# Stores of chunk preparation from GpSimd, and half of the retention's gate columns behind the z columns

## The chip, the cores and the metric

The kernel runs on one core of a Trainium2 chip. It is one program with one launch. The metric is the time of one execution on the device, in microseconds; the number compared is the median over runs. The engines are named TensorE (PE), VectorE (DVE), ScalarE (ACT), GpSimd (POOL) and SyncE (SP); SP computes nothing and only issues transfers.

## The reference

One layer of a diffusion backbone over 1024 latent tokens with 256 context tokens ahead of them, width 1024, all in float32:

```python
h = concat([modulate(rms_norm(ctx)), modulate(rms_norm(x))])          # 1280 tokens
p = h @ w_in                                                          # 4112 columns
qkv_a, z, ab, rq, rk, rv, rg = split(p)
qkv_a = silu(short_conv(qkv_a))                                       # 5 taps, q/k/v of the delta rule
q, k = l2_normalize(q) * 128 ** -0.5, l2_normalize(k)
o_gdn = rms_norm(delta_rule(fwd) + delta_rule(bwd)) * silu(z)         # 4 heads of 128, chunks of 64
o_ret = head_group_norm(retention(fwd) + retention(bwd)) * silu(rg)   # 4 heads of 128, rotary on rq, rk
x = x + g1 * (concat([o_gdn, o_ret])[latent] @ w_out)
x = x + g2 * swiglu(modulate(rms_norm(x)))
return rms_norm(x, final_g)
```

Inside the delta rule each chunk needs the solution of a unit lower triangular system:

```python
decay = where(incl, exp(G[i] - G[j]), 0)            # G: cumulated log gates of the chunk
A   = where(strict, (k * beta) @ k.T * decay, 0)
sol = triangular_solve(A + I, rhs)                  # per chunk, head and direction
qk  = (q @ k.T) * decay
```

The gate columns rg (512 of them) and z (512) are needed only behind the scans, as silu(rg) and silu(z).

## The kernel before

The kernel works on tiles of 128 tokens: 2 of the context and 8 of the latents, numbered 0 to 9, each with 4 heads and 2 directions. Matrix products of float32 are made of three products of a high and a low part (`whi`, `wlo`, `hhi`, `hlo`).

The stages in program order that matter here:

- **Column-major convolutions** (`conv_block`, matmuls in L611 to L613 into `b`, taps in L621 on VectorE, SiLU in L624 on ScalarE). One call makes 128 columns: blocks 4 to 7 are k, 0 to 3 are q, 8 to 11 are v. Between them `ada_rest` computes the rest of the adaLN vector. Its last calls write the gate rows with `SY.dma_start(grow[...], row)` (L506), behind an addition on VectorE (L505).
- **Token-major groups** (`token_major(g, ...)`, matmuls in L371 to L373 into `tm`). One group is 256 columns; groups 6 and 7 are the two halves of rg, groups 8 and 9 are z. Each works through the 8 latent tiles: 24 matmuls of 128x256 for a tile, then a finish on ScalarE (`fin_gate`, L532) and a store (L387). The weights of a group are two loads of 512 KB, split by ScalarE (L344) and VectorE (L345). Groups 6 and 7 take their weights from pool `W2` with loads issued by SyncE, groups 8 and 9 from pool `W` with loads issued by ScalarE. Behind `W2` come the pools of the next stage (`GU`, `GI`, `GP`), in the memory that it leaves.
- **Chunk preparation** (`pre(t)`). For a tile: load k (`kc`), its products (`kk`, L705), for latent tiles also q (`qc`), its transposes (`qt`) and products (`kq`, L715). For each direction ("a half" in what follows): load the broadcast gates (`gw`, two buffers, L718), cut them by an affine select on GpSimd (`e`, L722), four Exp on ScalarE (L726), the products `ut` and for latent tiles `sp` on VectorE (L730, L732), an Exp of `gw` (L735) and the product `sp` on GpSimd (L736), and two stores: `un<-ut` (L733) and `sd<-sp` (L737), both from SyncE.
- **Inversion** (`invert(b)`), for batches of 4, 4 and 2 tiles: load the 32x32 diagonal blocks (`yr`, L751), then 31 steps of two VectorE instructions each (L765, L767) on `X`, a transposing copy (`XT`, L769) and four stores to `xd`.
- **Merges** (`merge(b)`): load `U` and `t` (L783 to L788), then small matmuls (L807 to L834) that put the 32x32 inverses together to 128x128.
- v convolutions (each with transposes `vT`, L856, and scaled copies `vt`, L859) stand in the program between the solves of batches 0 and 1 and the preparation of batch 2; groups 8 and 9 follow merge 2; the scans come behind them.

The program order isn't the order on the engines. A scheduler orders the instructions of all engines ahead of time, by dependences, priorities and its own times, and each engine then runs its list strictly in order. So a change in the program moves instructions on every engine. All DMA issues are part of such a list too: an issue that waits holds up everything behind it on its engine.

```python
BATCH = [[0,1,2,9],[3,8,4,7],[5,6]]
```

## Time and profile before

| | us |
|---|---|
| median of 3 runs | 1476.58 (1475.48 to 1484.42) |
| the profiled execution | 1477.96 |
| its span | 1476.2 |
| TensorE busy | 1397.2 (95%) |
| VectorE busy | 964.6 (65%) |
| ScalarE busy | 614.0 (42%) |
| GpSimd busy | 590.3 (40%) |

The page splits the span into 40 slices of 36.9 us; a digit is the busy share of the slice in tenths. A row of the windows gives the stretch, its length, the busy time of the engines named (with the count of instructions), the granted clock of TensorE as a share of full speed, the busy share of the DMA engines and the GB/s. A row of the timeline gives the start in us, the length in us, the engine, the line, the operation, what it writes and reads, and in brackets how long the engine stood idle ahead of it and what ended that. A row of groups gives busy time and mean ns, then the idle time ahead of these instructions and what ended most of it. A row of waits gives the instruction that waited, what it waited for, the us in total, how often and the longest.

### The profile page before, as it was taken

How to read it: one execution, taken by the hardware profiler on the slowest of the kernel's cores; microseconds unless marked ns; L12 is line 12 of the kernel's file. 1: busy time of each engine (PE TensorE's matmuls, PEld its weight loads, DVE VectorE, ACT ScalarE, POOL GpSimd, SP SyncE). 2: the span in 40 equal slices, each digit the busy share in tenths (PEclk: the TensorE clock that was granted, in tenths of full speed). 3: DMA queues.
4: the chain of work that ended last, by engine and by line, in shares of the span. 5: the costliest groups of instructions: out<-in, count | busy, mean ns of one | idle time of the engine just before them, and what ended most of it. 6: DMA issues, size and time to landing. Idle time of an engine off the chain costs nothing.

```text
span 1476.2 us, 24111 instructions
## 1 busy us (share of the span) xinstructions
PE 1397.2 (95%) x8919; PEld 1199.2 (81%) x8919; DVE 964.6 (65%) x1856; ACT 614.0 (42%) x1326; POOL 590.3 (40%) x501
## 2 busy tenths in 40 slices
PE   7999999986789999899799899999999999999997
PEld 2898888975689999898688688877888888788885
DVE  6566789289792435689676877556555564657477
ACT  5643564587333111245443623233333332444445
POOL 0120010243202344234144688898555552335321
PEclk9999999998899999999899999999999999999999
DMA  9536686688888625996532265674222242776863
GB/s 337 197 105 205 189 249 200 219 264 277 282 216 277 238 76 178 416 341 209 184 125 104 97 238 210 242 264 162 105 97 105 107 151 79 260 260 194 288 216 114
DMA packets 170421, 298.14 MB, mean 202 GB/s; under 512 B 43496, under 2 KB 93880, under 8 KB 165952
## 3 DMA queue, kind: packets, MB, share of 16 engines
q1 hardware_dynamic: 118752, 253.17, 50.2%
q10 hardware_dynamic: 49072, 35.83, 7.8%
q0 software_dynamic: 2480, 7.60, 1.4%
q8 instruction: 70, 1.15, 0.3%
q14 instruction: 47, 0.39, 0.1%
HBM read 206.60 MB, written 89.96 MB: 201 GB/s over the span
## 4 chain that ended last, share of the span: by engine, by line
PE 55%; POOL 6%; DMA 5%; DVE 4%; issue 2%; ACT 2%; SPq 1%; ACTq 0%; POOLq 0%; DVEq 0%
PE ffn L1344 7%; PE ffn L1342 6%; PE ffn L1343 6%; PE fo L1470 4%; PE fo L1469 4%; PE fo L1468 4%; PE tm L371 3%; PE tm L373 3%; PE tm L372 3%; PE op L1203 2%; PE op L1201 2%; PE op L1202 2%; DMA wd<-tw 2%; POOL ws L1315 1%; DMA pk<-sd 1%
## 5 line engine op out<-in xcount | busy, mean ns | idle before, releaser
L371 PE MATMUL tm<-whi,hhi 128*128 128x256 f32 (+1 forms) x704 | 199.5, 287 | 7.7 <-ACT vt L859 3.4
L372 PE MATMUL tm<-wlo,hhi 128*128 128x256 f32 (+1 forms) x704 | 199.3, 285 | 2.4 <-issue 2.0
L373 PE MATMUL tm<-whi,hlo 128*128 128x256 f32 (+1 forms) x704 | 197.7, 285 | 0.0
L371 PEld LDWEIGHTS tm<-whi,hhi 128*128 128x128 f32 x704 | 132.8, 190 | 11.8 <-ACT vt L859 3.6
L1342 PE MATMUL ffn<-t,whi 128*128 128x512 f32 x352 | 136.9, 390 | 1.3 <-ACT whi L344 1.3
L1344 PE MATMUL ffn<-t,wlo 128*128 128x512 f32 x352 | 137.0, 390 | 1.0 <-DVE wlo L345 1.0
L1343 PE MATMUL ffn<-t,whi 128*128 128x512 f32 x352 | 137.0, 389 | 0.0
L372 PEld LDWEIGHTS tm<-wlo,hhi 128*128 128x128 f32 x704 | 133.7, 190 | 2.1 <-issue 0.9
L373 PEld LDWEIGHTS tm<-whi,hlo 128*128 128x128 f32 x704 | 132.8, 190 | 2.6 <-issue 1.8
L344 ACT ACTIVATE whi<-wraw 128x512 fp32r<-128x512 f32 (+2 forms) x98 | 75.1, 771 | 141.4 <-PE ffn L1343 80.5
L344 ACT ACTIVATE whi<-ws 128x512 fp32r<-128x512 f32 x88 | 55.6, 632 | 171.5 <-PE ffn L1343 123.4
L345 DVE TENSOR_TENSOR wlo<-ws,whi 128x512 fp32r<-128x512 f32 x88 | 93.9, 1068 | 47.0 <-ACT whi L344 46.8
L1469 PE MATMUL fo<-wlo,ahi 128*128 128x512 f32 x308 | 120.2, 390 | 2.1 <-DVE wlo L345 2.1
L1468 PE MATMUL fo<-whi,ahi 128*128 128x512 f32 x308 | 119.3, 390 | 0.7 <-ACT ahi L344 0.7
L1470 PE MATMUL fo<-whi,alo 128*128 128x512 f32 x308 | 119.0, 390 | 0.0
L345 DVE TENSOR_TENSOR wlo<-wraw,whi 128x512 fp32r<-128x512 f32 (+2 forms) x92 | 99.4, 1082 | 24.6 <-ACT whi L344 24.6
L1342 PE MATMUL ffn<-b,whi 128*128 128x512 f32 x264 | 103.8, 393 | 4.4 <-ACT whi L344 4.4
L1344 PE MATMUL ffn<-b,wlo 128*128 128x512 f32 x264 | 103.6, 393 | 0.8 <-DVE wlo L345 0.8
L1343 PE MATMUL ffn<-b,whi 128*128 128x512 f32 x264 | 103.4, 392 | 0.0
L612 PE MATMUL b<-hlo,whi 128*128 128x512 f32 (+1 forms) x256 | 94.4, 369 | 0.0
L613 PE MATMUL b<-hhi,wlo 128*128 128x512 f32 (+1 forms) x256 | 94.3, 368 | 0.0
L611 PE MATMUL b<-hhi,whi 128*128 128x512 f32 (+1 forms) x256 | 94.3, 368 | 0.0
(446 smaller groups left out, 3448.1 us busy)
## 6 DMA issues: line engine op xcount, KB each, us to landing
adaw<-ada SPq DMA_DIRECT2D x48, 512.0 KB, 4.4
pk<-sd SPq DMA_DIRECT2D x16, 1536.0 KB, 10.0
wraw<-wfi SPq DMA_DIRECT2D x44, 512.0 KB, 3.7
ar<-ad SPq DMA_DIRECT2D x33, 512.0 KB, 4.7
w<-wfo SPq DMA_DIRECT2D x22, 512.0 KB, 5.7
wd<-tw SPq DMA_DIRECT2D x11, 1024.0 KB, 4.8
ad<-act SPq DMA_DIRECT2D x20, 512.0 KB, 3.0
raw<-wd SPq DMA_DIRECT2D x20, 512.0 KB, 4.9
```

Source lines behind the costliest of these rows:

```text
L344: S.activation(hi, raw, AF.Copy)
L345: e.tensor_tensor(lo, raw, hi.bitcast(F32), ALU.subtract)
L371: T.matmul(o, hhi[:, k, tsl], whi[:, k % 4, :], start=(k == 0), stop=False)
L372: T.matmul(o, hhi[:, k, tsl], wlo[:, k % 4, :], start=False, stop=False)
L373: T.matmul(o, hlo[:, k, tsl], whi[:, k % 4, :], start=False, stop=(k == KT - 1))
L612: T.matmul(o, whi[:, k, :], hl, start=False, stop=False)
L1342: T.matmul(o, whi[:, k, :], xhi(xn, slice(0, 4), k), start=(first and k == 0), stop=False, **kw)
L1343: T.matmul(o, whi[:, k, :], xlo(xn, slice(0, 4), k), start=False, stop=False, **kw)
L1344: T.matmul(o, wlo[:, k, :], xhi(xn, slice(0, 4), k), start=False, stop=(k == 3), **kw)
L1468: T.matmul(po[g][i], ahi[:, ts], whi, start=(j == 0 and not kw), stop=False, **kw)
L1469: T.matmul(po[g][i], ahi[:, ts], wlo, start=False, stop=False, **kw)
L1470: T.matmul(po[g][i], alo[:, ts], whi, start=False, stop=(j == FH - 1), **kw)
```

## The change

Three things are changed. The gate row store of `ada_rest` is issued by GpSimd instead of SyncE. In `pre`, both stores of a half of a latent tile (t >= 2; 16 halves) are issued by GpSimd, behind its product `sp`; the stores of the 4 halves of the two context tiles stay on SyncE. Group 7, the second half of rg, leaves its place behind group 6, ahead of the chunk preparation, and follows groups 8 and 9; with that its weights come from pool `W`, loaded from ScalarE's queue.

```diff
@@ ada_rest
                 V.tensor_tensor(row, row, ps[:1, :], ALU.add)
-                SY.dma_start(grow[0 if c == 2 else 1][:, half * 512:(half + 1) * 512], row)
+                G.dma_start(grow[0 if c == 2 else 1][:, half * 512:(half + 1) * 512], row)
@@ behind the q convolutions
         checkpoint("q")
-        for g in (6, 7):
-            token_major(g, LAT, fin_gate, S, W2, SY)
+        token_major(6, LAT, fin_gate, S, W2, SY)
         checkpoint("rg")
@@ pre
-                SY.dma_start(un[b][:, 1 - d, c * H:(c + 1) * H, :], ut)
-                if t >= 2:
+                if t < 2:
+                    SY.dma_start(un[b][:, 1 - d, c * H:(c + 1) * H, :], ut)
+                else:
                     S.activation(gw, gw, AF.Exp)
                     G.tensor_tensor(sp[:, 1], gw, qc, ALU.mult)
-                    SY.dma_start(sd[t, :, 8 - 8 * d:10 - 8 * d], sp.rearrange("p a h i -> p a (h i)"))
+                    G.dma_start(un[b][:, 1 - d, c * H:(c + 1) * H, :], ut)
+                    G.dma_start(sd[t, :, 8 - 8 * d:10 - 8 * d], sp.rearrange("p a h i -> p a (h i)"))
@@ behind merge 2
-        for g in (8, 9):
+        for g in (8, 9, 7):
             token_major(g, LAT, fin_gate, S, W)
```

What this moves in the lists of three engines, at one place each. VectorE where the q convolutions end and the chunk preparation begins, before (`y` are taps, `row` is the gate row, `ut` and `sp` the products of preparation):

```order
L621 SCALAR_TENSOR_TENSOR y<-u,cw,y 128x254
L505 TENSOR_TENSOR row<-row,gr 1x512
L730 TENSOR_TENSOR ut<-kk,e 128x512 x6
L732 TENSOR_TENSOR sp<-kq,e 128x512 x2
L345 TENSOR_TENSOR wlo<-wraw,whi 128x8x128
L621 SCALAR_TENSOR_TENSOR y<-u,cw,y 128x1022
```

and the same place now:

```order
L505 TENSOR_TENSOR row<-row,gr 1x512
L345 TENSOR_TENSOR wlo<-wraw,whi 128x8x128
L621 SCALAR_TENSOR_TENSOR y<-u,cw,y 128x1022
L621 SCALAR_TENSOR_TENSOR y<-u,cw,y 128x1023
L621 SCALAR_TENSOR_TENSOR y<-u,cw,y 128x254
L621 SCALAR_TENSOR_TENSOR y<-u,cw,y 128x1023
L621 SCALAR_TENSOR_TENSOR y<-u,cw,y 128x255
L621 SCALAR_TENSOR_TENSOR y<-u,cw,y 128x1022
L621 SCALAR_TENSOR_TENSOR y<-u,cw,y 128x255
L729 TENSOR_TENSOR ut<-kk,e 128x512 x2
```

The taps of the first v convolution stand ahead of the first `ut` now. (Lines behind L684 are one lower or one higher in the new text.)

GpSimd in the preparation of the second batch, before (`e` is the affine select, `sp` the product):

```order
L722 AFFINE_SELECT e<-gw 128x512
L736 TENSOR_TENSOR sp<-gw,qc 128x512
L722 AFFINE_SELECT e<-gw 128x512 x2
L736 TENSOR_TENSOR sp<-gw,qc 128x512 x2
L722 AFFINE_SELECT e<-gw 128x512
```

and now, with the stores of `ut` and `sp` in its list:

```order
L721 AFFINE_SELECT e<-gw 128x512 x2
L736 TENSOR_TENSOR sp<-gw,qc 128x512
L737 DMA un_2657<-ut 128x512
L738 DMA sd<-sp 128x1024
L736 TENSOR_TENSOR sp<-gw,qc 128x512
L737 DMA un_2657<-ut 128x512
L721 AFFINE_SELECT e<-gw 128x512
L738 DMA sd<-sp 128x1024
L721 AFFINE_SELECT e<-gw 128x512
```

An affine select stands behind the stores of the half or two halves ahead of it.

TensorE where merge 2 begins, before (`m1` and `m2` are merge matmuls; `tm_5543` is a tile of the group behind z, all of groups 6 to 9 is done):

```order
L372 MATMUL tm_5543<-wlo_5537,hhi_86 128x256
L834 MATMUL m2_4772<-U1_4550,xt2_4773 64x64 x16
L807 MATMUL m1_4825<-t64_4815,U2_4813 32x32 x32
L373 MATMUL tm_5543<-whi_5536,hlo_87 128x256
L371 MATMUL tm_5543<-whi_5536,hhi_86 128x256
```

and now (`tm_5316` and `tm_5317` are the fifth and sixth of the 8 tiles of group 7):

```order
L371 MATMUL tm_5317<-whi_5192,hhi_86 128x256
L835 MATMUL m2_4536<-U1_4314,xt2_4537 64x64 x16
L808 MATMUL m1_4589<-t64_4579,U2_4577 32x32 x32
L372 MATMUL tm_5317<-wlo_5193,hhi_86 128x256
L373 MATMUL tm_5317<-whi_5192,hlo_87 128x256
```

Group 7 stands between the merges now, and what stood there comes behind merge 2.

## The prediction

> **What bounds the kernel now.** I read the page first, then busy time by stretch, then the stretch around the change on each engine, then what SyncE waits for.
>
> The page, its span and the two rows of the 40 slices for TensorE and its clock:
>
> ```profile
> span 1476.2 us, 24111 instructions
> PE 1397.2 (95%) x8919; PEld 1199.2 (81%) x8919; DVE 964.6 (65%) x1856; ACT 614.0 (42%) x1326; POOL 590.3 (40%) x501
> PE   7999999986789999899799899999999999999997
> PEclk9999999998899999999899999999999999999999
> ```
>
> TensorE is busy 95% of the span, so a change can win only what TensorE stands idle, or lose by making idle time. The weak slices are numbers 9 to 11 and the clock falls with them: 295 to 405 us. That is the chunk preparation. By 40 us:
>
> ```profile
> core 0: us, PE busy (x) PEld busy (x) DVE busy (x) ACT busy (x) POOL busy (x), PEclk, DMA share, GB/s
> 240.00:280.00 40.00, 40.00 (x299) 37.45 (x298) 21.01 (x41) 17.73 (x34) 6.80 (x9) 1.00 0.54 166
> 280.00:320.00 40.00, 38.17 (x232) 32.86 (x231) 25.93 (x33) 31.94 (x94) 15.26 (x14) 1.00 0.89 282
> 320.00:360.00 40.00, 31.54 (x186) 26.77 (x184) 39.48 (x60) 34.40 (x92) 18.73 (x16) 0.97 0.82 255
> 360.00:400.00 40.00, 25.56 (x188) 24.97 (x189) 31.38 (x68) 16.23 (x52) 10.02 (x8) 0.81 0.88 297
> 400.00:440.00 40.00, 34.45 (x891) 32.55 (x889) 37.02 (x97) 11.94 (x21) 0.95 (x1) 0.96 0.87 204
> 440.00:480.00 40.00, 37.77 (x636) 36.01 (x637) 12.93 (x35) 12.28 (x23) 7.81 (x17) 1.00 0.86 282
> 480.00:583.00 103.00, 103.00 (x879) 102.69 (x879) 44.40 (x138) 11.76 (x16) 45.77 (x91) 1.00 0.42 154
> ```
>
> TensorE's idle time from 280 to 480 us is 1.83 + 8.46 + 14.44 + 5.55 + 2.23 = 32.5 us; before (240 to 280) and after (480 to 583) there is none. So 32.5 us, and a few more for the clock of 0.81 and 0.96, is all the change can win. VectorE is full in 320 to 360 and nearly so in 400 to 440: its chain (preparation, inversion of three batches, merges) sets the pace, and TensorE waits for it.
>
> **What leaves the front.** TensorE and VectorE where group 7 ends and preparation begins:
>
> ```profile
> 276.06 0.28 PE L372 MATMUL tm<-wlo,hhi 128*128 128x256 f32 x1
> 276.17 0.28 PE L373 MATMUL tm<-whi,hlo 128*128 128x256 f32 x1
> 276.29 1.95 PE L705 MATMUL kk<-kc 128*128 128x128 f32 x16
> 261.10 0.68 DVE L505 TENSOR_TENSOR row<-row,gr 1x512 f32<-1x512 f32 x1 [1.84 <-PE gr L504]
> 277.48 1.29 DVE L730 TENSOR_TENSOR ut<-kk,e 128x512 f32<-128x512 f32 x2 [15.70 <-POOL X L755]
> 276.51 1.84 POOL L755 MEMSET X<- 128x1024 f32 x2 [7.06 <-PE tm L373]
> 268.53 2.46 ACT L726 ACTIVATE e<-e,nG 128x128 f32<-128x128 f32 x8 [1.46 <-POOL e L722]
> ```
>
> Group 7 is 8 token tiles x 8 k x 3 = 192 matmuls, 0.12 us apart: 23.0 us. While they run VectorE does nothing for 15.7 us, though the first two decay tiles e stand ready at 268.53 + 2.46 = 270.99; the first kk is queued behind group 7, and GpSimd's clearing of X (in memory that group 7's weights held) waits for it too, with the third decay tile behind it.
>
> In the new order the v convolution follows group 6 at once and the first kk stands 116 convolution matmuls later, at about 270 us. So the first ut comes at 271.5 instead of 277.5: **-6.0 us**. It can't come before e.
>
> **What has to be paid later.** The last steps of the first inversion, the first of the second, the end of the third, merge 2's first matmul and a weight split behind the third inversion:
>
> ```profile
> 380.78 0.19 DVE L767 TENSOR_TENSOR X<-X,tmp 128x31 f32<-128x31 f32 x1
> 389.32 0.20 DVE L765 TENSOR_TENSOR tmp<-L,X 128x31 f32<-128x31 f32 x1 [5.03 <-ACT L L758]
> 441.89 1.12 DVE L769 COPY XT<-X 64x1024 f32<-64x1024 f32 x1
> 457.38 0.75 PE L807 MATMUL m<-t,U 32*32 32x32 f32 x64
> 447.06 1.23 DVE L345 TENSOR_TENSOR wlo<-wraw,whi 128x1024 fp32r<-128x1024 f32 x1 [4.05 <-ACT whi L344]
> ```
>
> Counting TensorE's order up to the last matmul of merge 2, the new kernel has done the same work but 110 of the 128x256 matmuls fewer (112 fewer at its first): 110 x 0.12 = **13.2 us of debt**. After merge 2 TensorE is dense to 583 us, so everything behind moves by (shift of merge 2) + 13.2. Merge 2 must come 13.2 us sooner, at 444 us, to break even. Group 7 takes its other work along: two weight loads (now from ScalarE's queue, no longer SyncE's), two splits on VectorE, 8 gates and 8 stores on ScalarE. Two splits are 2.5 us of VectorE; they cost 0 where VectorE waits anyway (4.05 us ahead of this one), 2.5 inside an inversion. I take 0: ScalarE, 12 of 40 us busy from 400 to 480, has the room too.
>
> **How far the chain moves.** VectorE's pieces of the chain (stretch, its length, busy time, clock, DMA share, GB/s), then in the fifth and sixth row its convolution taps (L621) alone, before and in the first inversion, and its groups of ut and of the copies XT and L from 276 to 444 us, with the first and last ut:
>
> ```profile
> 262.00:277.00 15.00, 0.00 (x0) 1.00 0.59 176
> 277.00:312.00 35.00, 20.16 (x26) 1.00 0.83 263
> 314.00:381.00 67.00, 63.50 (x104) 0.87 0.84 271
> 389.00:415.00 26.00, 23.71 (x64) 1.00 0.93 247
> 416.00:443.00 27.00, 24.81 (x68) 0.94 0.87 223
> 276.00:314.00 38.00, 8.76 (x8) 1.00 0.82 259
> 314.00:381.00 67.00, 20.97 (x20) 0.87 0.84 271
> L730 DVE TENSOR_TENSOR ut<-kk,e 128x512 f32<-128x512 f32 x20 | 13.5, 685 | 30.9 <-POOL X L755 15.7 <-ACT e L726 7.0 <-DMA un<-ut 4.4
> L769 DVE COPY XT<-X 128x1024 f32<-128x1024 f32 (+1 forms) x3 | 4.4, 1469 | 0.1
> L759 DVE COPY L<-yr 64x1024 f32<-64x1024 f32 (+1 forms) x3 | 3.6, 1194 | 0.1
> L730 DVE TENSOR_TENSOR ut<-kk,e x20: 674/686/692, 277.5 to 373.5; 128x512 f32<-128x512 f32 x20
> ```
>
> The first inversion starts when batch 0 is prepared (314 us); VectorE is then full for 67 us, of which 20.97 are taps. In the new order the taps of the first two v convolutions, and some of the third's, stand ahead of that inversion: two and a bit of four (29.7 in all, 8.76 + 20.97). They run in the hole of 15.7 us and in the 35 - 20.16 = 14.8 us that VectorE idles from 277 to 312, so they are covered. About one convolution's taps, 29.7 / 4 = 7.4 us, leave the inversion: **-7.4**. The 5.03 us before the second inversion follow a late ACT queue, whose vt copies come sooner once the last v convolution does: I take **-5**, with 0 as the other end. ut and sp of batch 2 (four halves, two products of some 0.69 us each) move partly from the first inversion into the second: nothing in sum.
>
> **The stores.** What SyncE waited for from 276 to 475 us, and GpSimd's groups from 240 to 480 us, with its issues now:
>
> ```profile
> SPq L733 <- DVE ut L730: 29.2, 16, 4.3
> SPq L718 <- POOL sp L736: 6.0, 4, 4.5
> L736 POOL TENSOR_TENSOR sp<-gw,qc 128x512 f32<-128x512 f32 x16 | 22.9, 1435 | 16.7 <-ACT gw L735 8.9 <-issue 6.2 <-DMA sd<-sp 0.9
> L722 POOL TENSOR_SCALAR_AFFINE_SELECT e<-gw 128x512 f32<-128x512 f32 x20 | 15.8, 791 | 59.8 <-DMA gw<-grow_d 49.4 <-DVE y L621 4.3 <-DMA qc<-qd 3.6
> L387 POOL DMA_DIRECT2D rd<-res x36: 557/557/738, 458.1 to 583.1; - x36
> ```
>
> SyncE stops 29.2 us for ut with the loads of gw, kc, qc and yr behind it; these waits leave its queue. But the gw loads themselves waited on GpSimd's free buffer (6.0 us in 4 places), and e waits 49.4 us for gw to land with DMA at 0.82 to 0.89 busy, which no issuing engine changes. I credit **-3 us**, between 0 and those 6.0.
>
> The Trainium skill's page "DMA: Bandwidth & Descriptors", section "Issuing engines are not separate DMA queues", says that starting transfers from several engines saves only issue time; the 49.4 us behind DMA agree with it.
>
> On GpSimd 32 stores arrive (16 un, 16 sd): 32 x 0.557 to 0.738 = 18 to 24 us, beside a busy time of 15.3 + 18.7 + 10.0 = 44 of 120 us from 280 to 400. So there is room, and I cost it at 0; if it all lay on the chain, +18. What is queued behind a store that waits for ut is the next half's affine select and sp product. The store of the gate row, moved as well, waits for L505 (261.1 + 0.7 us) ahead of the first affine selects, which come 0.6 us and more before 268.53 now and wait for gw to land: 0.
>
> **Sum.** Chain: -6.0 - 7.4 - 5 - 3 = -21.4 us; debt +13.2; net **-8.2 us**. The profiled run took 1477.96 us (span 1476.2 and 1.8 around it), 1.4 above the median 1476.58, so 1477.96 - 8.2 = 1469.8 against its own time, 1468.4 against the median: I say 1468.5. Ends: without the -5 and the -3, 0 net, 1476.6 (with the splits 1479); with 5 more, of the 7.0 and 4.4 us that ut waited for e and for its buffer's store, 1463.
>
> **Rivals.** (About 1%, 14.8 us, is what counts as different from no change: below 1461.8 or above 1491.4.)
>
> *The chain closes up.* VectorE is busy 20.16 + 63.50 + 23.71 + 24.81 = 132 us of the 165 between 277 and 442. If its 33 us of idle go, as SyncE no longer stops and taps fill the gaps, the chain gains up to 6 + 33 + the 14 us of taps that go into the hole, but TensorE's 32.5 idle us cap the net at -32; half to five sixths of the way from the forecast to that cap is -20 to -28: 1448 to 1457. For: VectorE's 15.7 us hole is real and filled. Against: preparation waits for gw to land, and inversions run pair on pair at fixed length (26 us each).
>
> *GpSimd becomes the queue that holds everything (slower).* Each half now has on GpSimd 0.79 + 1.44 + 2 x 0.56 = 3.35 us, against 2.23; halves come every (373.5 - 277.5)/19 = 5.05 us. GpSimd stops for ut, which stands behind taps of some 1.05 us each (20.97 / 20) on VectorE, and with it the next half's affine select. If 1.1 us (the two issues) of each of the 16 halves falls on the chain, it loses 17.8: net +9.6, 1486; if the -5 and -3 fail too, +17.6, 1494. It decides from 8.2 / 16 = 0.5 us a half. For: the groups above show GpSimd waiting between its steps for ACT and VectorE. Against: the 36 rd stores that GpSimd issues now cost 0.557 at the median and 0.738 at most.
>
> The Trainium skill's page "SBUF — State Buffer", section "Who interferes with whom", speaks against this edit: it says that a VectorE copy or tensor_scalar keeps GpSimd from writing the descriptors of its own stores, and gives 620 ns alone and 3100 ns beside a copy. Here VectorE's copies are few (XT and L, 4.4 + 3.6 us, 6 instructions), so by that page some 6 x 2.5 = 15 us at the very worst, an estimate; the rd issues, which run beside no such copies, can't show it.
>
> *Nothing moves but the front.* The head start of 6 us passes unused into the wait for gw, and the chain stays as it is: -6.0 + 13.2 = +7, 1484. For: e waits for gw 49.4 us. Against: kk, X and e are all released by group 7's end.
>
> **Chances.** Forecast 0.5 (its own range 1460 to 1479), the closed-up chain 0.25, GpSimd's queue 0.18, only the front 0.07. Faster by over 1%: 0.08 of the forecast's + 0.23 of the second = 0.31. Slower: 0.12 of GpSimd's + 0.02 = 0.14. Within 1%: 0.55. The range that leaves out 2 in 10: 1450 (near the closed-up chain's end) to 1488 (half of GpSimd's case).
>
> **What the new profile would show.** First ut at about 271.5 us and taps on VectorE from 266 to 271; the first inversion's last step at 362 to 368; merge 2's first matmul at 436, and TensorE's last token-major matmul near 575 (now 583). SyncE no longer waiting for ut beyond the four stores left to it. On GpSimd the un and sd issues at 0.56 us. Wrong I would be if affine selects wait for stores (the GpSimd case), if the first inversion starts later than 308 us, or if the idle time of TensorE, moved, is the same 32.5 us plus the debt.

## The result and the profile after

The changed kernel takes 1493.98 us (median, 1493.26 to 1495.6); the kernel before, timed beside it, 1476.03 us. The ratio on record is 1.0106, with a 95% interval of 1.0086 to 1.0126 (the quotient of these two medians is 1.0122): slower by about 1%, where 1468.5 us had been forecast. The profiled execution has a span of 1493.8 us, 17.6 more than before. From here on "before" is that profile of 1476.2 us.

The page after: its span, the busy times, and TensorE with its clock in 40 slices (37.3 us each).

```profile
span 1493.8 us, 24119 instructions
PE 1409.9 (94%) x8919; PEld 1210.2 (81%) x8919; DVE 967.5 (65%) x1856; ACT 617.8 (41%) x1328; POOL 614.0 (41%) x537
PE   7999999977789999899699899999999999999997
PEclk9999999997889999999899999999999999999999
```

The same 8919 matmuls take 12.7 us more (1409.9 against 1397.2), and TensorE's idle time grows by 4.9 (1493.8 - 1409.9 = 83.9 against 79.0): together the 17.6 us. Where it is, by 40 us (the columns are those of the same view before):

```profile
240.00:280.00 40.00, 39.66 (x227) 33.42 (x227) 28.82 (x50) 21.59 (x41) 9.80 (x12) 1.00 0.64 191
280.00:320.00 40.00, 32.59 (x181) 28.19 (x180) 25.59 (x33) 31.38 (x94) 23.75 (x25) 0.88 0.78 245
320.00:360.00 40.00, 28.54 (x165) 25.34 (x165) 35.71 (x54) 32.44 (x95) 21.49 (x25) 0.78 0.78 253
360.00:400.00 40.00, 33.28 (x244) 32.68 (x243) 37.74 (x84) 17.16 (x39) 17.22 (x19) 0.87 1.05 308
400.00:440.00 40.00, 30.53 (x854) 28.82 (x853) 32.96 (x87) 11.43 (x20) 0.95 (x1) 0.91 0.79 229
440.00:480.00 40.00, 39.86 (x653) 38.18 (x652) 5.28 (x7) 14.32 (x28) 0.00 (x0) 0.96 0.75 246
480.00:583.00 103.00, 103.00 (x881) 103.00 (x880) 44.14 (x137) 9.64 (x12) 48.35 (x96) 1.00 0.38 136
```

From 240 to 480 us TensorE idles 0.34 + 7.41 + 11.46 + 6.72 + 9.47 + 0.14 = 35.5 us; it was 32.5. It idles earlier now, and in more of the rows: 280 to 320 loses 7.41 us where it lost 1.83. And the clock is below 1 in five rows where it was in three. Busy time times (1 - clock), row by row, is 3.91 + 6.28 + 4.33 + 2.75 + 1.59 = 18.9 us; before 0.95 + 4.86 + 1.38 = 7.2. So by this accounting 3.0 us of idle and 11.7 us of slower clock, 14.7 of the 17.6 us, are lost up to 480 us. Each figure is from one execution. Three kernels below that take the same time as the one before (e9, e17 and e18) lose 11.1, 9.4 and 11.7 us to the clock by the same accounting, so 2 to 5 of the 11.7 us more are no sign of a longer time.

VectorE's chain after, at the places named in the prediction (first `ut`, first copy L with the first inversion's first step, that inversion's last step, the second's first step, the third's copy XT), and TensorE's first matmul of merge 2:

```profile
271.58 1.28 DVE L729 TENSOR_TENSOR ut<-kk,e 128x512 f32<-128x512 f32 x2
...
311.77 1.04 DVE L760 COPY L<-yr 64x1024 f32<-64x1024 f32 x1 [5.71 <-DMA yr<-un]
312.91 0.21 DVE L766 TENSOR_TENSOR tmp<-L,X 128x31 f32<-128x31 f32 x1
...
373.09 0.19 DVE L768 TENSOR_TENSOR X<-X,tmp 128x31 f32<-128x31 f32 x1
...
377.16 0.20 DVE L766 TENSOR_TENSOR tmp<-L,X 128x31 f32<-128x31 f32 x1
...
435.12 1.03 DVE L770 COPY XT<-X 64x1024 f32<-64x1024 f32 x1
458.75 0.75 PE L808 MATMUL m<-t,U 32*32 32x32 f32 x64
```

The first `ut` stands 5.9 us earlier (277.48 before), the first inversion's end 7.7 (380.78), the second's start 12.2 (389.32), the third's XT 6.8 (441.89), and merge 2 1.4 us later (457.38).

### The profile page after: what moved, and what is told of

It is laid out like the page before. It is cut to its first block, busy times and chain, and to the rows that moved or that the text cites. A ratio compares the mean times of both kernels' runs of the same rounds, so it can differ in the third digit from the quotient of the medians.

```text
span 1493.8 us, 24119 instructions
## 1 busy us (share of the span) xinstructions
PE 1409.9 (94%) x8919; PEld 1210.2 (81%) x8919; DVE 967.5 (65%) x1856; ACT 617.8 (41%) x1328; POOL 614.0 (41%) x537
## 4 chain that ended last, share of the span: by engine, by line
PE 57%; DMA 13%; DVE 10%; POOL 8%; issue 7%; ACT 4%; SPq 0%; ACTq 0%; POOLq 0%; DVEq 0%
PE ffn L1345 6%; PE ffn L1343 6%; PE ffn L1344 6%; PE tm L373 5%; PE tm L372 5%; PE tm L371 5%; DMA ar<-ad 3%; PE b L611 2%; PE b L612 2%; PE b L613 2%; DVE wlo L345 2%; PE op L1202 2%; PE op L1204 2%; PE op L1203 2%; DMA wd<-tw 2%
## 5 line engine op out<-in xcount | busy, mean ns | idle before, releaser
L345 DVE TENSOR_TENSOR wlo<-wraw,whi 128x512 fp32r<-128x512 f32 (+2 forms) x92 | 100.1, 1090 | 29.3 <-ACT whi L344 29.2
```

Source lines behind the costliest of these rows:

```text
L345: e.tensor_tensor(lo, raw, hi.bitcast(F32), ALU.subtract)
```

## The experiments

Two questions: why the chain to merge 2 gained nothing, and what each of the two parts does alone. The table has all kernels that ran. Its columns: the ratio to the kernel before, with its interval; by how much, in the profile, the first step of the first inversion is later than before (314.17); by how much merge 2 is done later (473.52); the debt, which is the 128x256 matmuls that stand behind merge 2 now and stood ahead of it before, times 0.12 us; the sum of the last two; and the shift of the whole span (1476.2). All but the ratio are read from one execution of each kernel.

| kernel | ratio | first inversion | merge 2 done | debt | sum | span |
|---|---|---|---|---|---|---|
| changed kernel | 1.0106 [1.0086, 1.0126] | -1.3 | +0.3 | 13.2 | 13.5 | 17.6 |
| e1_move_only | 1.0073 [1.0046, 1.0100] | -3.3 | -5.2 | 16.0 | 10.8 | 13.9 |
| e2_stores_only | 1.0145 [1.0113, 1.0177] | +10.5 | +25.1 | -1.7 | 23.4 | 22.3 |
| e3_g7_mid | 1.0053 [1.0027, 1.0079] | +2.2 | +8.0 | 5.3 | 13.3 | 10.1 |
| e4_g7_first | 1.0073 [1.0048, 1.0099] | -4.1 | -11.9 | 16.0 | 4.1 | 6.2 |
| e5_un_only | 1.0038 [1.0020, 1.0055] | +3.2 | +12.4 | 0.2 | 12.6 | 8.1 |
| e6_sd_only | 1.0066 [1.0040, 1.0091] | +5.1 | +14.4 | 0 | 14.4 | 15.2 |
| e7_split | 1.0056 [1.0035, 1.0078] | +0.3 | +8.2 | 5.2 | 13.4 | 8.6 |
| e8_warm | 1.0159 [1.0134, 1.0184] | +0.7 | +6.4 | 23.0 | 29.4 | 21.1 |
| e9_pool_busy | 1.0006 [0.9992, 1.0020] | +2.8 | +3.8 | 0 | 3.8 | 3.8 |
| e10_g7_v4 | 1.0081 [1.0054, 1.0109] | -4.0 | +6.1 | 5.6 | 11.7 | 9.7 |
| e11_g7_v3 | 1.0090 [1.0054, 1.0125] | +1.7 | +13.2 | 7.4 | 20.6 | 15.8 |
| e12_sd_act | 1.0110 [1.0094, 1.0127] | +8.2 | +15.4 | 0.6 | 16.0 | 17.4 |
| e13_g7_fill | 1.0032 [1.0017, 1.0047] | -1.2 | +11.2 | -1.7 | 9.5 | 12.2 |
| e14_gw_g | 1.0076 [1.0051, 1.0101] | +5.6 | +16.6 | -1.2 | 15.4 | 16.9 |
| e15_stores_gw_g | 1.0144 [1.0110, 1.0179] | +11.3 | +31.4 | -3.1 | 28.3 | 28.3 |
| e16_after_gw_g | 1.0119 [1.0090, 1.0147] | +11.1 | +14.4 | 9.6 | 24.0 | 20.1 |
| e17_pool_each | 1.0014 [0.9999, 1.0029] | +1.7 | +5.3 | 0 | 5.3 | 2.4 |
| e18_grow_only | 0.9992 [0.9974, 1.0011] | +0.4 | +5.0 | 0 | 5.0 | 0.1 |

Three things to read from it first. Sum and span agree within 5 us in all but e8: that a kernel pays the shift of merge 2 plus the debt was the prediction's rule, and it holds to that accuracy. In e9, e17 and e18, which cost nothing that can be measured, merge 2 is done 3.8 to 5.3 us later all the same, so a shift of this size says nothing by itself. And no kernel beats the one before.

### The two parts apart

e1, the move alone:

```diff
-        for g in (6, 7):
-            token_major(g, LAT, fin_gate, S, W2, SY)
+        token_major(6, LAT, fin_gate, S, W2, SY)
...
-        for g in (8, 9):
+        for g in (8, 9, 7):
```

> Only group 7 is moved behind groups 8 and 9; all stores are SyncE's as before. Theory A (the loss is group 7's 23 us leaving the front: TensorE stands idle just as long in the chunk preparation, 35 instead of 32 us from 240 to 480 us, at a lower clock, and pays the debt behind): +12 to +18 us, about 1490. Theory B (the loss is GpSimd's queue, with its stores between affine selects: halves every 6.7 us instead of 5.9): within 6 us of before, 1470 to 1482, or faster.

e2, the stores alone (the gate row's, and both stores of the latent halves), group 7 in its old place:

```diff
-                SY.dma_start(grow[0 if c == 2 else 1][:, half * 512:(half + 1) * 512], row)
+                G.dma_start(grow[0 if c == 2 else 1][:, half * 512:(half + 1) * 512], row)
...
+                    G.dma_start(un[b][:, 1 - d, c * H:(c + 1) * H, :], ut)
+                    G.dma_start(sd[t, :, 8 - 8 * d:10 - 8 * d], sp.rearrange("p a h i -> p a (h i)"))
```

> Only the stores are GpSimd's (un and sd of latent tiles, the gate rows); group 7 stays behind group 6. Theory A: within 4 us of before, 1472 to 1480. Theory B: +10 to +18 us, 1486 to 1494.

Each part alone makes the kernel slower: the move by 0.73%, the stores by 1.45%. e1 is slower by 10.8 us by the ratio and 12.8 by the medians, the lower edge of theory A, though with 31.9 us of idle from 240 to 480 and not 35. The stores cost 21 us, more than theory B's 18, with 48.1 us of idle. Together the two parts cost 1.06%, less than the stores alone: they don't add. With the move the first inversion starts 3.3 us early; with the stores 10.5 us late; with both 1.3 early. Why the stores delay it so much less once group 7 is gone wasn't tested.

What SyncE waited for in e2, and then in e1, from 276 to 475 us (the instruction that waited, what for, us in total, times, longest):

```profile
SPq L718 <- POOL sp L737: 42.8, 11, 8.2
```

```profile
SPq L732 <- DVE ut L729: 29.6, 13, 4.6
...
SPq L717 <- POOL sp L735: 8.7, 7, 3.1
```

In e1, with the stores on SyncE, that engine still stops 29.6 us for `ut`. In e2 that wait is nearly gone, and in its place stand 42.8 us in which the loads of `gw` wait for GpSimd's product `sp` to free their buffer (6.0 us before). The wait wasn't taken out of SyncE's list; the next entry took it up. It was to be seen whether that new wait is what the stores cost.

### What about the stores costs time

e5 moves the `un` stores alone to GpSimd, e6 the `sd` stores alone:

```diff
-                    SY.dma_start(sd[t, :, 8 - 8 * d:10 - 8 * d], sp.rearrange("p a h i -> p a (h i)"))
+                    G.dma_start(sd[t, :, 8 - 8 * d:10 - 8 * d], sp.rearrange("p a h i -> p a (h i)"))
```

> The kernel before with one thing changed: the 16 un stores of latent tiles issued by GpSimd behind its product, all else as before. With all stores moved, two un issues of batch 0 came 4.6 and 3.2 us behind their ut (0.7 before), because they stand in GpSimd's list behind a product and an affine select; yr could be loaded 7.4 us later, and the first inversion began 10.5 us later. Theory B1 (the loss of the stores is un's late issue ahead of yr): +6 to +15 us, first inversion 5 to 10 us later. Theory B2 (it is GpSimd's time in sum, 0.55 us for each store, that slows the halves): half of the loss of all stores, +8 to +12. Theory B3 (the loss is that both U loads, 4 MB, were issued together and the second inversion waited 11.7 us): within 4 us of before.

> The kernel before with the 16 sd stores alone issued by GpSimd; nobody reads them before the scans. Theory B1: within 4 us of before. Theory B2: +8 to +12 us. Theory B3: within 4 us of before.

0.38% and 0.66%: the `sd` stores, which no inversion reads, cost at least as much as those whose data the inversion loads. So lateness of the `un` stores themselves isn't the whole cost. e5 (5.6 us, the inversion 3.2 later) falls just short of theory B1 and of B2, and is outside B3; e6 (9.7 us) is B2's size alone, and B2 is what the next two runs test. SyncE's list where batch 0's last `un` store (301.43 before, 304.56 in e6) is followed by the loads `yr`, before and then in e6 (start, length):

```profile
301.43 0.32 SPq L733 DMA_DIRECT2D un<-ut  x1
302.58 0.32 SPq L718 DMA_DIRECT2D gw<-grow_d  x1
302.99 0.38 SPq L737 DMA_DIRECT2D sd<-sp  x1
303.43 0.42 SPq L664 DMA_DIRECT2D qc<-qd  x1
304.06 4.49 SPq L751 DMA_DIRECT2D yr<-un  x4
```

```profile
303.70 0.32 SPq L718 DMA_DIRECT2D gw<-grow_d  x1
304.08 0.42 SPq L664 DMA_DIRECT2D qc<-qd  x1
304.56 0.42 SPq L733 DMA_DIRECT2D un<-ut  x1
311.07 4.24 SPq L751 DMA_DIRECT2D yr<-un  x4
```

With the `sd` store gone, a `gw` and a `qc` load come up ahead of the last `un` store, and `yr` follows that store after 6.5 us instead of 2.6. That order is seen; that it makes the store land late is an inference, since the loads and the store weren't swapped alone.

e9 leaves all stores on SyncE and adds useless work on GpSimd behind each `sp` product (four clears of a tile that nothing reads):

```diff
                     G.tensor_tensor(sp[:, 1], gw, qc, ALU.mult)
+                    for _ in range(4):
+                        jk = GP.tile([P, 128], F32, tag="jk", name="jk", bufs=1)
+                        G.memset(jk, 0.0)
```

> The kernel before, all stores SyncE's, and 4 memsets of a 128x128 scratch tile by GpSimd behind each of the 16 products sp (useless work, about 1 us a half, as the two store issues take). If the stores' loss is GpSimd's time between its steps of preparation (theory B2): +10 to +20 us. If it is the way the stores take (late issue, another queue) and not the time: within 5 us of before.

The ratio is 1.0006, but the clears depend on nothing and all 64 ran from 248.2 to 296.0 us, ahead of most halves. So e9 says little. e17 has the useless work read `sp`, so that it can't run before its half:

```diff
                     G.tensor_tensor(sp[:, 1], gw, qc, ALU.mult)
+                    for _ in range(3):
+                        jk = GP.tile([P, P], F32, tag="jk", name="jk", bufs=1)
+                        G.tensor_tensor(jk, sp[:, 1, 0], sp[:, 1, 0], ALU.mult)
```

> The kernel before, and three useless 128x128 products on GpSimd behind each of the 16 sp products; they read sp and write a tile that nothing reads. In e9 the useless clears depended on nothing and 64 of 64 ran from 248 to 296 us, ahead of most halves, so e9 loaded GpSimd only at the start of the preparation. These products can't run before their half: by a quarter of the 1.44 us of the full product they take some 0.36 us each, about 1.1 us a half, which is what two store issues take. All stores and loads stay on SyncE. Theory P (GpSimd's time in each half lies on the chain): ratio 1.006 to 1.012, first inversion 3 to 6 us later, as the runs with moved issues. Theory O (it is the order of the issues that costs, not GpSimd's time): 0.998 to 1.003.

Their row in e17 (duration in ns, first and last start), and their group from 276 to 475 us (busy us, mean ns):

```profile
L739 POOL TENSOR_TENSOR jk<-sp x48: 393/408/1362, 289.9 to 380.5; 128x128 f32<-128x128 f32 x48
...
L739 POOL TENSOR_TENSOR jk<-sp 128x128 f32<-128x128 f32 x48 | 25.6, 534 | 3.0
```

25.6 us, 1.6 a half, spread from 289.9 to 380.5 us, against 18.3 for the 32 store issues; and the ratio is 1.0014, 1.0029 at the top. Theory P falls: the time that GpSimd is busy isn't the cost. e17 leaves open another thing: an issue on GpSimd also waits for its data, and everything behind it in the list waits too. Ahead of the moved stores GpSimd stands idle for 19.6 us in e5, 14.6 in e6 and 20.0 in the changed kernel, and no run tells how much of that falls on the chain. e18 takes the third part of the stores, the gate row's, alone:

```diff
-                SY.dma_start(grow[0 if c == 2 else 1][:, half * 512:(half + 1) * 512], row)
+                G.dma_start(grow[0 if c == 2 else 1][:, half * 512:(half + 1) * 512], row)
```

> The kernel before with the gate row's stores alone issued by GpSimd (one line; the un and sd stores and group 7 stay). Nothing is left out. The un stores alone cost 0.38%, the sd stores alone 0.66%, all three 1.45%. If the parts add, this one gives 1.002 to 1.006; the prediction costed it at 0: 0.999 to 1.001. A change of the order of four lists alone, with no issue in the preparation itself moved, would cost here if it is the scheduler's new order that costs.

0.9992: nothing, as costed. `un` and `sd` together cost 1.45%, one by one 0.38 and 0.66; the difference is no more than the intervals allow, and it isn't the gate row's. e12 turns the question round, the `sd` stores from ScalarE's queue:

```diff
-                    SY.dma_start(sd[t, :, 8 - 8 * d:10 - 8 * d], sp.rearrange("p a h i -> p a (h i)"))
+                    S.dma_start(sd[t, :, 8 - 8 * d:10 - 8 * d], sp.rearrange("p a h i -> p a (h i)"))
```

> The kernel before with the 16 sd stores issued by ScalarE. With sd issued by GpSimd, batch 0's last un took 6.5 us from its issue to yr's first load (2.6 before). Theory Q (a bulky store from any other queue runs beside un, which otherwise lands ahead of it): the same stretch is 5 us or more, and the time +4 to +12 us. Theory G (only GpSimd's stores do that): the stretch stays at 2 to 3.5 us. The time alone can't tell them apart, since ScalarE's own queue stops for the product sp.

1.10%: more than on GpSimd, and more than theory Q's 12 us. The stretch that Q and G differ in is 6.7 us (the last `un` of batch 0 at 304.96, `yr` at 311.62), as Q has it: a `gw` and a `qc` load come up ahead of that `un` here too. So the cost isn't GpSimd's alone; it comes, at least in part, with taking the store off SyncE's list.

Last, the wait for `gw` itself. e14 has GpSimd issue the 16 `gw` loads of the latent halves in the kernel before, e15 in e2, e16 in the changed kernel:

```diff
-                SY.dma_start(gw.rearrange("p h i -> p (h i)"),
+                (G if t >= 2 else SY).dma_start(gw.rearrange("p h i -> p (h i)"),
```

> The kernel before, with one edit: the 16 loads of the broadcast gates (gw) of the latent halves are issued by GpSimd instead of SyncE. GpSimd runs the product that frees the buffer, so the load waits for nothing there; the four loads of the context tiles stay on SyncE. Nothing is left out of the computation. In the kernel before, SyncE waits only 6.0 us for these buffers. Theory W (SyncE's in-order list is conserved: what one removed wait frees is taken up by the next entry that waits): SyncE still stops about 29 us for ut in front of everything else, so the time stays within 6 us of before, ratio 0.996 to 1.004. Rival V (any DMA issue put on GpSimd between its steps delays the preparation): 16 issues of 0.56 us, as many as in the run that moved the sp stores alone, so about the same cost, ratio 1.006.

> Only the stores moved to GpSimd (group 7 in its old place), and with it the 16 loads of gw of the latent halves issued by GpSimd too. Nothing is left out. The stores alone gave a ratio of 1.0145 and SyncE then waited 42.8 us for the buffers of gw. Theory W: that wait is the cost; with the loads off SyncE's list it is gone, yr, kc and qc are no longer queued behind it, and the ratio falls to 1.000 to 1.005, with the first inversion's first step back at 314 to 318 us (324.7 with the stores alone). Rival V: GpSimd has 48 issues instead of 32, so the cost rises, ratio 1.015 to 1.021, and the first inversion starts at 325 us or later.

> The changed kernel, and with it the 16 loads of gw of the latent halves issued by GpSimd too. Nothing is left out. There SyncE waited 40.1 us for the buffers of gw. Theory W: that wait goes, what is queued behind it comes sooner, and the chain to merge 2 gains some of the 21.4 us that were predicted; the debt of about 13 us remains. Ratio 1.000 to 1.008, below the 1.0106 of the changed kernel. Rival V: 48 issues on GpSimd instead of 32, ratio 1.011 to 1.018. If it is as slow as the changed kernel, 1.009 to 1.012, the wait for gw was one that costs nothing there.

All three went against theory W: 1.0076, 1.0144 and 1.0119, where it had 0.996 to 1.004, 1.000 to 1.005 and 1.000 to 1.008. SyncE's waits in e15:

```profile
SPq L664 <- POOL sp L737: 63.8, 6, 13.7
```

The wait for `gw` is gone from SyncE, and 63.8 us stand at L664 in its stead: loads through the helper there, that of `qc` among them, whose buffer the same product frees. So the replacement went one entry further (29.2, 42.8, 63.8 us), and the time didn't fall. Rival V, that any DMA issue put on GpSimd costs, had the bounds of e16 and, for e14, 1.006 (measured from 1.0051 up); and in e15 the first inversion starts at 325.5 us, as V said. But in e15 48 issues cost no more than 32 in e2, e17 shows that it can't be GpSimd's busy time, and e12 costs 1.10% with no issue moved there. Neither theory stands whole. What the runs have in common is the place. In the six kernels that, with group 7 in its old place, take `un`, `sd` or `gw` issues of the latent halves off SyncE (e2, e5, e6, e12, e14, e15) the first inversion starts 3.2 to 11.3 us later, and merge 2 is done 12.4 to 31.4 us later, in the same order but for e12; in the three that leave those issues where they are (e9, e17, e18) it is 0.4 to 2.8, and 3.8 to 5.3. A delay at the first inversion isn't carried on to merge 2 as it is; in these six it grows. The ways to that place differ: in e6 and e12 the stretch from the last `un` of batch 0 to `yr` is 6.5 and 6.7 us, in e14 it is 2.4 and the last `ut` itself is late (306.95 against 300.71).

### Where group 7 stands

e4 puts it ahead of groups 8 and 9, e7 splits it (tiles 0 to 3 in the old place, 4 to 7 behind), e3, e11 and e10 put it behind the second, third and fourth v convolution, e13 behind the preparation of batch 1 and ahead of the v convolutions. The stores stay on SyncE in all of them.

```diff
# e4
+        for g in (7, 8, 9):
# e7
+        token_major(7, LAT[:4], fin_gate, S, W2, SY)
...
+        token_major(7, LAT[4:], fin_gate, S, W)
# e3 (h == 1), e11 (h == 2), e10 (h == 3)
             conv_block(8 + h, y, False)
+            if h == 1:
+                token_major(7, LAT, fin_gate, S, W)
# e13
         solve(1)
+        token_major(7, LAT, fin_gate, S, W)
```

> Stores as before; group 7 stands in the program behind the second v convolution, so that TensorE's list has its 192 matmuls among the preparation of batches 0 and 1, where the changed kernel's TensorE stood idle for 5.65 and 7.70 us, and VectorE still gets the first v taps early. Theory A: the preparation has its filler, so idle of 240 to 480 us falls by 5 to 15 us and the time is 1462 to 1472. If what counts is only that the first kk waits for less (the place of the filler does not matter): as the move alone. Theory B: 1470 to 1480.

> Stores as before; group 7 stands in the program behind the merges but ahead of groups 8 and 9. The work and its amount behind the preparation are those of the move alone, only the names of the filler differ: it is to show how much the order of otherwise equal work, and the schedule made anew, is worth. Both theories: within 3 us of the move alone.

> Stores as before; only the last four of group 7's eight tiles are moved behind groups 8 and 9, the first four stay. The debt at merge 2 is 43 matmuls, 5.2 us (110 in the changed kernel). If the end is the shift of merge 2 plus the debt, and the first ut still comes 5 us sooner, merge 2 comes 3 to 8 us sooner and the time is 1474 to 1481, -3 to +3 us. If any move of group 7 costs the clock, +5 to +10.

> Stores as before; group 7 stands in the program behind the fourth v convolution, so that its matmuls lie in TensorE's list between the chunk products of tiles 7 to 10, behind all v convolutions: where the move alone stood idle for 10 to 15 us from 320 to 360 us. Debt at merge 2: 47 matmuls, 5.6 us. If merge 2's shift plus the debt sets the time and the chain keeps what it won in the two moves alone (merge 2's end 5 to 12 us sooner): -6 to +1 us, 1471 to 1478. If VectorE's chain is slowed by whatever TensorE does there: +5 to +10.

> As the run before, with group 7 behind the third v convolution: its matmuls come ahead of the fourth. Debt 62 matmuls, 7.4 us; the fourth convolution's taps come some 14 us later than in the move alone. Merge 2 later than with group 7 behind the fourth; +2 to +10 us.

> Stores as before; group 7 stands in the program behind the preparation and inversion of batches 0 and 1 and ahead of the v convolutions, with weights from the other pool, so that it fills TensorE's list ahead of and among the first chunk products without holding them back (the first kk has some 50 of its matmuls behind it). Debt at merge 2: -14 matmuls, -1.7 us. If a filler costs nothing as long as it stands where the chain can't start yet, and the chain starts 4 to 6 us sooner: 1466 to 1475, the only version here that could beat the kernel before. If any filler among the chunk products holds the chain back as much as it fills: within 3 us of before, or slower.

None comes to the time before. Of what had been expected, e3's second case and e4's (as e1), e7's second (+5 to +10) and e13's last (or slower) came true; e10 and e11 cost 12 and 13 us, more than the 10 at which their ranges end; no version won. They trade one term for the other: e1 and e4 keep the chain short (merge 2 done 5.2 and 11.9 us sooner) and owe 16.0; e3, e7, e10, e11 and e13 owe 7.4 or less and have merge 2 done 6.1 to 13.2 us later. TensorE in e4 and then e10, by 40 us (busy, clock, DMA share, GB/s):

```profile
320.00:360.00 40.00, 25.21 (x158) 0.83 0.89 288
...
400.00:440.00 40.00, 33.08 (x781) 0.91 0.72 215
```

```profile
320.00:360.00 40.00, 31.36 (x226) 0.91 0.86 272
...
400.00:440.00 40.00, 27.56 (x678) 0.79 0.92 226
```

In e10 group 7 does fill 320 to 360 (6.15 us more busy), and 400 to 440 loses 5.52 of it: the last `ut` comes at 385.87 there, at 373.60 in e4; chunk products stand among and behind group 7 in TensorE's list.

### Idle that is filled with useless work

e8 is e1 with 64 useless 128x512 matmuls, eight ahead of the q transposes of each latent tile, into a bank that nothing reads. It was to tell whether the clock's loss goes when TensorE is kept at work.

```diff
             if t >= 2:
+                dm = bank_a("dm")
+                for _ in range(8):
+                    T.matmul(dm, hhi[:, 0, 0:P], hhi[:, 0, 0:512], start=True, stop=True)
```

> The move alone, and 64 useless matmuls of 128x512 (8 for each latent tile of the preparation, 0.233 us each, 14.9 us; their bank is never read). It computes more than is asked; the outputs are the same. If TensorE's idle time in the preparation is free and idleness is what lowers the granted clock: clock of 280 to 480 us above 0.95 and a time at or below that of the move alone, 1480 to 1491. If the extra work is simply added: 1500 to 1506.

1.59%, the time of "simply added" (median 1502.5 us), with 39.4 us of idle (31.9 in e1): the scheduler put most of them elsewhere. Their row in e8 (duration in ns, then first and last start):

```profile
L708 PE MATMUL dm<-hhi x64: 387/395/775, 248.3 to 377.8; 128*128 128x512 f32 x64
```

48 of the 64 start from 248.3 to 261.5, in a stretch where e1's TensorE had almost no idle to fill (0.44 us from 240 to 280), and the other 16 from 372.7 to 377.8. So this run settles nothing about the clock; that the 11.7 us follow from how the idle time is spread isn't shown.

## Why the prediction was wrong

**The step that failed** is the sum of the chain, -21.4 us at merge 2. It measured +1.4 at merge 2's first matmul and +0.3 at its last. The debt, +13.2, was right and was paid in full. 13.5 of the 17.6 us are so accounted for; where the other 4.1 arise behind merge 2 wasn't followed. Two readings in that sum failed: that the taps put ahead of the first inversion are covered, and that what VectorE gains is passed on to merge 2.

**First ut -6.0: right as a size, wrong as a term.** -5.9 measured. But the last `ut` of batch 0 came only 3.3 us sooner (297.37 against 300.71), and the first inversion's first step 1.3 (312.91 against 314.17). "If the first inversion starts later than 308 us" had been named as a sign of being wrong. VectorE, after, around the last two `ut` of batch 0 (the second and fourth row):

```profile
288.26 6.99 DVE L621 SCALAR_TENSOR_TENSOR y<-u,cw,y 128x1022 f32<-128x1022 f32 x4 [3.80 <-ACT y L615]
295.18 0.68 DVE L729 TENSOR_TENSOR ut<-kk,e 128x512 f32<-128x512 f32 x1
295.78 1.66 DVE L621 SCALAR_TENSOR_TENSOR y<-u,cw,y 128x1023 f32<-128x1023 f32 x2
297.37 0.68 DVE L729 TENSOR_TENSOR ut<-kk,e 128x512 f32<-128x512 f32 x1
```

The `e` of these two were done at 290.59 and 294.06 on ScalarE and their `kk` at 286.09 on TensorE, but taps of the next v convolution stand ahead of both in VectorE's list, and their input came late (3.80 us). So the taps weren't covered by idle time: the two `ut` start 4.6 and 3.3 us behind their `e`. From the last `ut` to the inversion's first step it is then 15.5 us instead of 13.5, with 5.71 of waiting for `yr<-un` in the row of the copy L above. The rival "nothing moves but the front" is nearest to this: the head start was lost, to the taps and not to the wait for `gw`. Its sum of +7 still counted the -6.0 that it called unused; without it, it is the debt alone.

**Taps leaving the first inversion -7.4: right as a size**, though part of them went ahead of the last `ut`, as just seen. VectorE's taps (L621) between the inversion's first and last step, after; they were 20.97 in 314 to 381 before:

```profile
313.00:373.00 60.00, 12.91 (x12) 0.80 0.83 263
```

8.1 us fewer, and the inversion takes 60.0 us (312.91 to 372.87, the start of its last pair of steps) instead of 66.4.

**The wait before the second inversion -5: right.** From the first inversion's last pair of steps to the second's first it is 4.29 us (372.87 to 377.16), 4.5 less than the 8.76 before. At that point the chain stands at -12.2.

**SyncE's credit -3: wrong, and in kind.** What SyncE waited for in the changed kernel from 276 to 475 us:

```profile
SPq L717 <- POOL sp L736: 40.1, 9, 8.0
...
SPq L752 <- DMA un<-ut: 7.2, 2, 4.1
...
SPq L733 <- DVE ut L729: 3.7, 2, 2.8
```

The 29.2 us for `ut` went, as said, but 40.1 came in front of `gw`. The prediction had seen these waits (6.0 us in four places) and read them as what would remain. It had asked what stood behind a store on GpSimd, and not what would next come up on SyncE. That this 40.1 us is the cost isn't shown: e15 and e16 took it off and gained nothing. The 49.4 us for `gw` to land, taken as a wait that no issuing engine changes, aren't fixed either: the same group waits 23.4 us after (row of L721 below). And 21.3 of the 49.4 lay ahead of 276 us, where the DMA share was 0.54: from 276 to 475 us it was 28.1.

**GpSimd's 32 issues at 0: right as far as time on the engine goes.** The groups after, on GpSimd from 240 to 480 us:

```profile
L721 POOL TENSOR_SCALAR_AFFINE_SELECT e<-gw 128x512 f32<-128x512 f32 x20 | 18.5, 924 | 27.3 <-DMA gw<-grow_d 23.4 <-DVE ut L729 3.8
L737 POOL DMA_DIRECT2D un<-ut x16 | 9.4, 587 | 7.8 <-DVE ut L729 6.0 <-DVE tmp L766 1.8
L738 POOL DMA_DIRECT2D sd<-sp x16 | 8.9, 555 | 12.2 <-DVE X L768 6.0 <-issue 3.1 <-DVE sp L731 1.4
```

0.587 and 0.555 us each, 18.3 in all, as taken from the 36 `rd` stores; and e17's useless work, longer than the issues, costs nothing that can be measured. The rival "GpSimd becomes the queue" had two parts. That the issues' time falls on the chain is what e17 speaks against. That GpSimd stops at a store for `ut` or `sp`, with the next half's affine select behind it, is seen: 7.8 and 12.2 us of idle ahead of the stores in these rows. How much of that is on the chain is open; e14, whose issues wait 3.0 us in all, costs 0.76% as well. So the rival's 1494 us is the measured time, but not by terms that the runs confirm: there is luck in it.

How large the price of 0 should have been depends on what it is added to. The stores alone cost 1.45%, 21 us (0.0145 x 1476); behind the move they add 0.33% (1.0106 against 1.0073, with intervals that overlap), some 5 us. It was costed as an engine's time, and not as a change in the order of in-order lists. Most of what the forecast missed is there without the stores: by the prediction's terms the move alone should have given -5.2 us (its sum without the -3), and e1 is 0.73% slower, some 11 us.

The Trainium skill's page "SBUF — State Buffer" gives 620 ns for a transfer that GpSimd issues when it runs alone and 3100 ns beside a VectorE copy, in the section "A bandwidth-pool intuition that's wrong (but worth ruling out)". The changed kernel can't show it: none of its 32 issues ran beside one of VectorE's copies, and none of the issues took longer than 617 ns. In the kernel before, two of the `rd` issues (484.92 and 486.67 us) ran beside a VectorE copy after all, `S<-up`, and took 0.559 us each, against a median of 0.557; that copy reads the result of a matmul, and no run has an issue beside a copy like XT.

**The chain behind the second inversion: missing.** The prediction carried the gain to merge 2 without following the pieces between. They gave 13.5 us back, from -12.2 to +1.4. The second inversion takes 1.9 us more (27.43 against 25.47) and the third 1.8 (25.68 against 23.90), and from XT to merge 2's first matmul it is 23.6 us instead of 15.5. VectorE around the third inversion (407.90 to 433.98) and behind it:

```profile
428.23 1.23 DVE L345 TENSOR_TENSOR wlo<-wraw,whi 128x1024 fp32r<-128x1024 f32 x1 [0.57 <-ACT whi L344]
...
433.98 1.23 DVE L345 TENSOR_TENSOR wlo<-wraw,whi 128x1024 fp32r<-128x1024 f32 x1
435.12 1.03 DVE L770 COPY XT<-X 64x1024 f32<-64x1024 f32 x1
449.26 0.69 DVE L832 TENSOR_SCALAR xt<-m 128x512 f32<-128x512 f32 x1 [13.10 <-PE m L831]
454.54 0.69 DVE L832 TENSOR_SCALAR xt<-m 128x512 f32<-128x512 f32 x1 [4.59 <-PE m L831]
```

A weight split stands inside the third inversion and another between its last step and XT, where before none stood. Behind XT it is VectorE that waits for TensorE, 17.7 us for the products of merge 1 (before, its copies `xt` waited 1.4 us for TensorE from 276 to 480 us in all). The last load of merge 2's inputs is issued only 2.1 us sooner than before (448.09 against 450.23), and from 440.14 us to merge 2 TensorE has no gap: from XT on it does 98 of the 128x256 matmuls and 318 of the merges', where it did 88 and 128 before, also without a gap. So merge 2 waits there not for the third inversion but for the work ahead of it in TensorE's list. By the accounting above TensorE had lost 14.7 us more, so the 13.2 us of work that it no longer had to do bought nothing. One of its idle stretches shows how the lists hang together:

```profile
311.75 1.06 ACT L759 ACTIVATE L<-yr 64x1024 f32<-64x1024 f32 x1 [5.07 <-DMA yr<-un]
314.86 0.79 PE L611 MATMUL b<-hhi,whi 128*128 128x512 f32 x1 [5.65 <-ACT y L615]
```

ScalarE's copy L waits for `yr`, the L615 that empties the convolution's bank stands behind it, and TensorE waits for that.

**"The idle time of TensorE, moved, is the same 32.5 us plus the debt"** was the last sign named. It came close: 35.5 us, moved 20 to 40 us forward. The "few more" that the prediction put beside the idle time, for the clock of the kernel before, are 7.2 us by the accounting above; that they could grow, to 18.9, was no term of its sum.

**Splits at 0: the other end came.** Two splits of 1.23 us stand before XT now, as in the rows above: the 2.5 us "inside an inversion". Which group's weights they split isn't told by the rows.

**Still open:** what a single issue costs that leaves SyncE's list. It is 0.38 to 1.45% for five choices of which issues and two engines; it isn't the time that an engine is busy with it, and no one wait explains it. The scheduler orders all engines anew for each of these kernels, so no run moves an issue and nothing else (in e9, e17 and e18, which move no issue of the preparation, the new order costs 0.14% at most by the ratio). A third buffer for `gw`, which would take that wait away without moving a load, wasn't tried. And the chance of "slower", 0.14, was too small for a change whose gain had to pass through five in-order lists and whose debt was certain.

## What to carry to other kernels

Work that fills an engine ahead of a stalling stretch is a debt at once when it is moved behind it; the gain has to be followed through every in-order list to the point where it is paid, link by link, before it may be set against the debt. When an issue that waits is taken out of an in-order list, look for the next entry that will wait in its place (here the loads whose two buffers a slower engine frees): its small wait of now is no measure of its wait then. And price a moved DMA issue by what it reorders and what has to wait behind it, not by the half microsecond that it takes.

## What the runs showed of the hardware

Idle time of about the same size came with different losses to the clock, from 240 to 480 us: 32.5 and 7.2 us in the kernel before, 31.3 and 11.7 in e18, which takes the same time, 35.5 and 18.9 in the changed one. TensorE by 20 us, in the changed kernel, where it idles (busy, clock, DMA share, GB/s):

```profile
340.00:360.00 20.00, 14.68 (x86) 0.64 0.91 280
360.00:380.00 20.00, 18.30 (x154) 1.00 1.06 353
380.00:400.00 20.00, 14.99 (x90) 0.74 1.04 263
400.00:420.00 20.00, 14.59 (x420) 0.83 0.88 240
```

Three stretches with 5.0 to 5.4 us of idle each have a clock of 0.64, 0.74 and 0.83; before, a stretch of 340 to 360 with 4.9 us had 0.95, and the lowest clock, 0.62, was in one of 11.1 us (360 to 380). So the clock isn't given by the idle time of a stretch alone, and no run here says by what.

A GpSimd that is busy 1.6 us longer in each of 16 halves cost nothing that can be measured (1.0014), while one issue of 0.59 to 0.60 us on average in each cost 0.38 to 0.76% (e5, e6, e14): the second also changes which transfer stands ahead of which, and waits for its data.
